# ConvFFN way down of a two-layer decoder trunk: block products in another order, accumulators of their own, and the next gate half placed ahead

## The chip, the cores and the metric

The kernel runs on one core of a Trainium2 chip. The metric is the device time of one execution in microseconds. A difference of 0.2% is about what a measurement of this kernel can tell from none.

## What is computed

Two decoder layers run over 512 positions of width 1024. Each layer adds three things to `x`: a mixer, a cross-attention, and a ConvFFN. Only the ConvFFN is touched by the change:

```python
def conv_ffn(h, w_up, conv_w, conv_b, w_down):
    S = h.shape[1]
    u = h @ w_up
    shift = lambda t, n: jnp.pad(t, ((0, 0), (n, 0), (0, 0)))[:, :S]
    u = sum(conv_w[CONV_WIDTH - 1 - n] * shift(u, n) for n in range(CONV_WIDTH)) + conv_b
    gate, up = jnp.split(u, 2, axis=-1)
    return (jax.nn.silu(gate) * up) @ w_down

    for l in range(DEPTH):
        ...
        x = x + conv_ffn(rms_norm(x, norm_ffn[l]), ffn_w_up[l], ffn_conv_w[l], ffn_conv_b[l], ffn_w_down[l])
```

The hidden width is 2816, that is 22 chunks of 128. All data are float32.

## The kernel before

**Arithmetic.** TensorE multiplies in a rounded 32-bit format. To keep float32 accuracy every operand is held as a high part (a ScalarE cast, line 213 for the helper `split`, line 171 for whole weight tiles) and a low part (VectorE subtracts the high part from the value, lines 214 and 172), and every product is three matmuls: high by high, high by low, low by high. Activations lie transposed: 128 features on the partitions, 512 positions along the row.

**The ConvFFN (`ffn`, line 578).** The 22 hidden chunks are worked in three parts of 8, 8 and 6 chunks. Inside a part the chunks come in pairs `m` (so a part has n = 4, 4 or 3 pairs). For each pair:

- the gate half: a weight tile of 1024 by 256 is loaded and split (`wload`), 2 times 24 matmuls of 512 columns go into one PSUM bank each (tag `pj`, 3 banks), and each bank is taken out by VectorE (line 585) and goes through the convolution: one ScalarE instruction (line 587) and two VectorE ones (588, 590), then the SiLU on ScalarE (601);
- the value half: the same with other weights, and a VectorE product with the gate (606);
- `seven` (line 314): from the two finished chunks it makes the seven right-hand factors of a seven-product block scheme for 2 by 2 blocks. Four VectorE instructions make sums (318 to 321), and `split` makes high and low parts in three steps: slot 0, slots 1 and 2, slots 3 to 6 of the tiles `s7h` and `s7l`.

**The way down (`seven_resid`, line 327).** After the pairs of a part the product with `w_down` follows, for two units `u` of 512 output features each. A unit loads two raw weight tiles (tag `wraw`, two buffers, shared with every other weight load), and makes seven weights out of them: `w11`, `w12` and `w22` are blocks of the raw tiles, `w1`, `w2`, `w4` and `w3` are sums, made by VectorE (`add`, line 348) in the tile `wsum` or in place. Each is split into parts held in the tiles `whi` and `wlo` (two buffers each, and each buffer holds two weights). A weight times its slot is a block product: `product` (line 350) issues 6n matmuls of 256 columns (line 357). With n = 4 a product is 24 matmuls, a unit 168 and a part 336; with n = 3 it is 18, 126 and 252. Over both layers the way down has 1848 of these matmuls.

The products go into three PSUM accumulators `al`, `be` and `de`, all with the tag `pj`. `into` (line 360) adds an accumulator to `x` with VectorE (line 362). The source order of a unit is w11 (al), w12 (be), w1 (de), w2 (al), w4 (de), w3 (al), w22 (al). The accumulator `al` keeps summing over four products, and is read by `into` after each of them, so the next matmul into `al` waits until that reading is over.

**What sets the order.** The code is written in source order and a scheduler then fixes, ahead of time, one order for each engine. Each engine works its own list strictly in that order and waits on semaphores where data or a buffer come from another engine. SyncE (SP) issues the weight loads. At the end of a part TensorE's list runs straight from the last value half to the first product of the way down, while the last pair's `seven` is still to be made.

**Names.** The profile's `wraw`, `whi`, `wlo`, `wsum`, `s7h`, `s7l`, `s7t`, `xT` (the residual `x`), `fu` and `fa` (the convolution's two tiles), and `ps_pj`, `ps_at`, `ps_ov`, `ps_tr` (PSUM banks by tag) are the program's own.

Of the kernel before, what the change touches and what calls it, by code (L numbers as in the profile page):

```python
# [33 lines left out]
def trunk(ctx, tc, x, mem, positions, norm_mix, norm_cross, norm_mem, norm_ffn,  # L34
# [292 lines left out]
    def seven_resid(w, r0, xs, u, tp, sums, after=None):  # L327

        n = len(xs)
        nk = 2 * n  # L330
        raws = []
        for i in range(2):
            raw = tl(wp, [P, KC, WCOL], "wraw", 2)
            SY.dma_start(out=raw[:, :nk], in_=wcols(w, r0, nk * P, (4 * u + 2 * i) * P))
            raws.append(raw)
        a11, a12 = (raws[0][:, i:nk:2] for i in range(2))
        a21, a22 = (raws[1][:, i:nk:2] for i in range(2))

        def parts():
            return tl(wp, [P, KC, WCOL], "whi", 2, FP32R), tl(wp, [P, KC, WCOL], "wlo", 2, FP32R)  # L340

        def put(t, i, src):
            h, lo = t[0][:, i * n:(i + 1) * n], t[1][:, i * n:(i + 1) * n]
            split(src, h, lo)
            return h, lo

        def add(out, a, b):
            V.tensor_tensor(out=out, in0=a, in1=b, op=ALU.add)  # L348

        def product(o, wt, slot, first):  # L350
            wh, wl = wt
            for j in range(2):
                c = slice(j * P, (j + 1) * P)
                for k in range(n):
                    xh, xl = xs[k][0][:, slot], xs[k][1][:, slot]
                    for i, (a, b) in enumerate(((wh, xh), (wh, xl), (wl, xh))):
                        T.matmul(o[:, j], lhsT=a[:, k, c], rhs=b, start=first and j == 0 and k == 0 and i == 0,  # L357
                                 stop=j == 1 and k == n - 1 and i == 2, skip_group_check=True)

        def into(i, th, o, op):  # L360
            x = xT2[2 * u + i][:, :, 256 * th:256 * th + 256]
            V.tensor_tensor(out=x, in0=x, in1=o, op=op)  # L362

        ta = parts()
        w11, w12 = put(ta, 0, a11), put(ta, 1, a12)
        ws = tl(tp, [P, KC // 2, WCOL], "wsum", sums)[:, :n]
        add(ws, a21, a22)
        al = ps("pj", 2, WCOL)
        product(al, w11, 0, True)
        be = ps("pj", 2, WCOL)  # L370
        product(be, w12, 1, True)
        tb = parts()
        w1 = put(tb, 0, ws)
        add(ws, ws, a11)
        w2 = put(tb, 1, ws)
        into(0, 0, al, ALU.add)
        into(0, 0, be, ALU.add)
        de = ps("pj", 2, WCOL)
        product(de, w1, 3, True)
        into(1, 1, de, ALU.subtract)  # L380
        product(al, w2, 4, False)
        into(0, 1, al, ALU.add)
        tc_ = parts()
        add(ws, ws, a12)
        w4 = put(tc_, 0, ws)
        add(a21, a11, a21)
        w3 = put(tc_, 1, a21)
        product(de, w4, 2, False)
        into(0, 1, de, ALU.add)
        product(al, w3, 5, False)  # L390
        into(1, 1, al, ALU.subtract)
        if after is not None:
            for c in (4 * u, 4 * u + 1):
                after(c)
        td = parts()
        w22 = put(td, 0, a22)
        product(al, w22, 6, False)
        into(1, 0, al, ALU.subtract)
        if after is not None:
            for c in (4 * u + 2, 4 * u + 3):  # L400
                after(c)
# [176 lines left out]
    def ffn(l, xp, sp):  # L578
# [14 lines left out]

        hs = {}

        def up_pair(m):
            gt = [None, None]

            def evg(j, o):
# [669 lines left out]
```

## Time and profile before

| | |
|---|---|
| median of 3 runs | 1644.17 us (1643.62 to 1646.21) |
| the profiled execution's own time | 1643.91 us |
| its span in the trace | 1642.2 us |
| TensorE (PE) busy | 1585.4 us, 97% |
| VectorE (DVE) busy | 1167.5 us, 71% |
| ScalarE (ACT) busy | 760.4 us, 46% |
| GpSimd (POOL) busy | 200.6 us, 12% |
| DMA | 145.71 MB, mean 89 GB/s |

The span goes from the first to the last instruction that the profiler saw; 1.7 us of the execution's own time lie outside it. PE's busy time says little by itself, since the ends of matmuls are modelled and overlap their successors. What counts is the distance from one matmul's start to the next one's: that is the pace, and whatever is above it is lost.

### The profile page before, as it was taken

The numbers are of one execution on the slowest core, as the hardware profiler recorded it, in microseconds if no ns is written. First come the engines' busy times: TensorE is split into PE (matmuls) and PEld (weight loads), VectorE is DVE, ScalarE is ACT, GpSimd is POOL, SyncE is SP. The second block draws the span as 40 slices with busy tenths as digits, with TensorE's granted clock in tenths as the row PEclk, the third lists the DMA queues.
The fourth block names the chain that finished last, engine by engine and source line by source line (L and its number), as shares of the span: only waits on it lengthen the run. The fifth ranks groups of instructions, "written<-read, shape, count | busy, mean of one in ns | idle before, by whom it ended". The sixth has DMA issues, their size and how long they took to land.

```text
span 1642.2 us, 23185 instructions
## 1 busy us (share of the span) xinstructions
PE 1585.4 (97%) x9182; PEld 1365.8 (83%) x9182; DVE 1167.5 (71%) x1888; ACT 760.4 (46%) x1312; POOL 200.6 (12%) x307
## 2 busy tenths in 40 slices
PE   8999999999998999998999999999999999998997
PEld 7977898887888888887789888988888879888877
DVE  6666966556788688688777676645564987787786
ACT  6576865444443443344433343543553543443342
POOL 3301421002000000001422223101011000000000
PEclk9999999999999999999999999999999999999999
DMA  6211433213222431311422123342112313221413
GB/s 189 78 53 35 128 104 125 78 52 103 77 77 71 135 103 52 129 64 39 129 78 78 52 79 102 103 154 92 63 52 77 103 58 129 96 78 54 152 39 90
DMA packets 144489, 145.71 MB, mean 89 GB/s; under 512 B 2844, under 2 KB 143837, under 8 KB 144381
## 3 DMA queue, kind: packets, MB, share of 16 engines
q1 hardware_dynamic: 143882, 143.98, 27.4%
q8 instruction: 73, 1.20, 0.3%
q0 software_dynamic: 96, 0.07, 0.1%
q14 instruction: 35, 0.29, 0.1%
q10 hardware_dynamic: 403, 0.18, 0.0%
HBM read 142.12 MB, written 2.10 MB: 88 GB/s over the span
## 4 chain that ended last, share of the span: by engine, by line
PE 85%; DVE 8%; ACT 3%; DMA 2%; issue 1%; POOL 1%; SPq 0%; ACTq 0%; DVEq 0%
PE ps_pj L184 22%; PE ps_pj L183 22%; PE ps_pj L185 22%; PE ps_pj L357 8%; DVE wlo L214 2%; PE ps_at L1091 2%; DVE xT L362 1%; DVE wsum L348 1%; DVE wlo L172 1%; ACT whi L213 1%; DVE s7l L214 1%; PE ps_ov L962 1%; DMA wraw<-in_ffn_w_down_dram 1%; DMA wraw<-in_ab_w_in_dram 1%; PE ps_tr L951 1%
## 5 line engine op out<-in xcount | busy, mean ns | idle before, releaser
L184 PE MATMUL ps_pj<-xl,whi 128*128 128x512 f32 x1088 | 433.4, 399 | 0.0
L183 PE MATMUL ps_pj<-xh,whi 128*128 128x512 f32 x1024 | 407.8, 399 | 0.0
L185 PE MATMUL ps_pj<-xh,wlo 128*128 128x512 f32 x1024 | 406.5, 398 | 0.0
L172 DVE TENSOR_TENSOR wlo<-wraw,whi 128x1024 fp32r<-128x1024 f32 (+1 forms) x228 | 266.1, 1199 | 42.7 <-ACT whi L171 42.1
L171 ACT CAST whi<-wraw 128x1024 fp32r<-128x1024 f32 (+1 forms) x228 | 219.6, 1013 | 139.7 <-PE ps_pj L184 94.2
L184 PEld LDWEIGHTS ps_pj<-xl,whi 128*128 128x128 f32 x1088 | 205.1, 188 | 47.2 <-issue 1.2
L183 PEld LDWEIGHTS ps_pj<-xh,whi 128*128 128x128 f32 x1024 | 193.1, 189 | 46.4 <-issue 1.2
L185 PEld LDWEIGHTS ps_pj<-xh,wlo 128*128 128x128 f32 x1024 | 192.9, 188 | 43.7
L357 PE MATMUL ps_pj<-s7h,whi 128*128 128x256 f32 x616 | 177.2, 290 | 17.3 <-DVE xT L362 8.2
L357 PE MATMUL ps_pj<-s7l,whi 128*128 128x256 f32 x616 | 175.7, 286 | 6.9 <-DVE s7l L214 6.9
L357 PE MATMUL ps_pj<-s7h,wlo 128*128 128x256 f32 x616 | 174.0, 286 | 5.6 <-DVE wlo L214 5.2
L357 PEld LDWEIGHTS ps_pj<-s7h,whi 128*128 128x128 f32 x616 | 118.0, 192 | 24.3 <-ACT s7h L213 8.8
L357 PEld LDWEIGHTS ps_pj<-s7l,whi 128*128 128x128 f32 x616 | 118.2, 192 | 9.7 <-DVE s7l L214 9.4
L357 PEld LDWEIGHTS ps_pj<-s7h,wlo 128*128 128x128 f32 x616 | 117.6, 192 | 7.7 <-DVE wlo L214 7.6
L246 POOL TENSOR_TENSOR nacc<-nacc,nsq 128x512 f32<-128x512 f32 x36 | 52.1, 1446 | 550.2 <-ACT nsq L245 549.8
L185 PE MATMUL ps_pj<-whi,xl 128*128 128x256 f32 x416 | 118.8, 288 | 0.1
L587 ACT ACTIVATE fa<-fu,ccol 128x512 f32<-128x512 f32 x88 | 71.6, 813 | 85.0 <-DVE fu L585 84.7
L585 DVE TENSOR_TENSOR fu<-ps_pj,rb 128x512 f32<-128x512 f32 x88 | 60.8, 691 | 62.9 <-PE ps_pj L185 62.8
L184 PE MATMUL ps_pj<-ol,whi 128*128 128x512 f32 x256 | 101.8, 398 | 0.0
L185 PE MATMUL ps_pj<-oh,wlo 128*128 128x512 f32 x256 | 101.4, 397 | 0.0
L183 PE MATMUL ps_pj<-oh,whi 128*128 128x512 f32 x256 | 100.0, 401 | 1.4 <-DVE xl L450 0.9
L362 DVE TENSOR_TENSOR xT<-xT,ps_pj 128x512 f32<-128x512 f32 x84 | 57.5, 685 | 43.9 <-PE ps_pj L357 43.7
(366 smaller groups left out, 2959.0 us busy)
## 6 DMA issues: line engine op xcount, KB each, us to landing
wraw<-in_ffn_w_up_dram SPq DMA_DIRECT2D x44, 1024.0 KB, 5.1
wraw<-in_xa_w_kv_dram SPq DMA_DIRECT2D x16, 1024.0 KB, 5.9
wraw<-in_ffn_w_down_dram SPq DMA_DIRECT2D x16, 1024.0 KB, 5.1
wraw<-in_hgrn_w_in_dram SPq DMA_DIRECT2D x16, 1024.0 KB, 5.4
wraw<-in_ab_w_in_dram SPq DMA_DIRECT2D x8, 1024.0 KB, 5.3
wraw<-in_xa_w_q_dram SPq DMA_DIRECT2D x8, 1024.0 KB, 5.2
wraw<-in_xa_w_o_dram SPq DMA_DIRECT2D x8, 1024.0 KB, 5.0
wraw<-in_ffn_w_down_dram SPq DMA_DIRECT2D x8, 768.0 KB, 4.4
```

What stands on the lines that cost most here:

```text
L171: A.copy(out=hi[:, k, c], in_=raw[:, k, c])
L172: V.tensor_tensor(out=lo[:, k, c], in0=raw[:, k, c], in1=f32(hi[:, k, c]), op=ALU.subtract)
L183: mm = T.matmul(o, lhsT=lh, rhs=rh, start=first, stop=False)
L184: T.matmul(o, lhsT=lh, rhs=rl, start=False, stop=False)
L185: T.matmul(o, lhsT=ll, rhs=rh, start=False, stop=last)
L214: V.tensor_tensor(out=lo, in0=src, in1=f32(hi), op=ALU.subtract)
L246: (V if c == KC - 1 else G).tensor_tensor(out=self.acc, in0=self.acc, in1=sq, op=ALU.add)
L357: T.matmul(o[:, j], lhsT=a[:, k, c], rhs=b, start=first and j == 0 and k == 0 and i == 0, stop=j == 1 and k == n - 1 and i == 2, skip_grou ...
L362: V.tensor_tensor(out=x, in0=x, in1=o, op=op)
L585: V.tensor_tensor(out=u, in0=o, in1=rb, op=ALU.mult)
L587: A.activation(out=a, in_=u, func=AF.Identity, scale=conv_col(l, 2, ch), bias=bias_col(l, ch))
L1091: T.matmul(po, lhsT=km[:, r * P:(r + 1) * P], rhs=skew(QP, h + r * P, (256 - h, 2), (2 * h, n2 // 2), (1, h)), start=True, stop=True)
```

## The change

- One function `seven_part` does both units. It has one order of products for most units ("fill") and another for the first unit of a layer's last part. In the fill order the products go w11 (al), w1 (de), w2 (al), w4 (de), w3 (al), w12 (be), w22 (al); in the other one w11 and w12 leave out their last pair at first, do it next, and then come w2, w1, w3, w4, w22.
- The accumulators get tags of their own: `al` has `at` (2 banks), `be` has `ov` (1 bank), `de` keeps `pj`. These tags were there before for attention's tiles.
- Inside a product the loop over pairs (k) is now outside and the one over the two column halves (j) inside. The matmul's line is 349 in the changed kernel (357 before), that of `into` is 366, that of `add` 353.
- A unit's first raw tile has a tile of its own, `wr`, with one buffer; the second still uses `wraw`. Splits of weights follow one another in pairs into a `whi` and `wlo` buffer over both units, so that a part takes 7 such buffers in a row where it took 8.
- The gate half of the next part's first pair is issued between the last value half and the way down. This holds for 4 of the 6 ways down; the last part of each layer has no next part.
- The tile `fa` has 6 buffers (4 before), `s7h` and `s7l` 4 (5 before).

The numbers of matmuls, casts, subtractions, sums, `into` instructions and loads stay the same. The diff, cut to its core:

```diff
-    def seven_resid(w, r0, xs, u, tp, sums, after=None):
+    def seven_part(w, r0, xs, sp, sums, fill, after=None):
...
+        def weights(src):
+            if side[1] == 0:
+                side[0] = tl(wp, [P, KC, WCOL], "whi", 2, FP32R), tl(wp, [P, KC, WCOL], "wlo", 2, FP32R)
+            h, lo = (t[:, side[1] * n:(side[1] + 1) * n] for t in side[0])
+            side[1] = 1 - side[1]
             split(src, h, lo)
             return h, lo
...
-            for j in range(2):
-                c = slice(j * P, (j + 1) * P)
-                for k in range(n):
-                    xh, xl = xs[k][0][:, slot], xs[k][1][:, slot]
...
+            for k in range(n) if ks is None else ks:
+                xh, xl = xs[k][0][:, slot], xs[k][1][:, slot]
+                for j in range(2):
+                    c = slice(j * P, (j + 1) * P)
...
+        def unit(u, fill):
+            raws = []
+            for i in range(2):
+                raw = tl(sp if i == 0 else wp, [P, KC, WCOL], "wr" if i == 0 else "wraw", 1 + i)
...
+            al, be, de = ps("at", 2, WCOL), ps("ov", 2, WCOL), ps("pj", 2, WCOL)
+            w11 = weights(a11)
+            if not fill:
+                w12 = weights(a12)
+                product(al, w11, 0, True, range(n - 1))
+                product(be, w12, 1, True, range(n - 1))
+                product(al, w11, 0, True, range(n - 1, n))
+                product(be, w12, 1, True, range(n - 1, n))
...
+                add(a21, a11, a21)
+                w3 = weights(a21)
+                w4 = weights(ws)
...
+            else:
+                add(ws, a21, a22)
+                w1 = weights(ws)
+                product(al, w11, 0, True)
+                product(de, w1, 3, True)
...
+                product(al, w3, 5, False)
+                w12 = weights(a12)
+                into(0, 1, de, ALU.add)
+                product(be, w12, 1, True)
+                w22 = weights(a22)
+                into(1, 1, al, ALU.subtract)
+                into(0, 0, be, ALU.add)
+            product(al, w22, 6, False)
...
+        unit(0, fill)
+        unit(1, True)
...
+        gt = gate_half(0)
         for a, b in parts:
             for m in range(a // 2, b // 2):
-                up_pair(m)
-            for u in range(2):
-                seven_resid(ffn_w_down[l], a * P, [hs[m] for m in range(a // 2, b // 2)], u, sp, 2 - l,
-                            (lambda c: store(sp, c)) if l == 1 and b == FC else None)
+                value_half(m, gt)
+                gt = gate_half(m + 1) if 2 * m + 2 < FC else None
+            seven_part(ffn_w_down[l], a * P, [hs[m] for m in range(a // 2, b // 2)], sp, 2 - l, gt is not None,
+                       (lambda c: store(sp, c)) if l == 1 and b == FC else None)
```

What this does to the engines' lists is seen at three places. The first is TensorE at the start of layer 0's first way down. Before, the last matmuls of the value half (512 columns) are followed at once by the product with `w11`:

```order
L184 MATMUL ps_pj_5114<-xl7_4515,whi_5075 128x512
L185 MATMUL ps_pj_5114<-xh7_4514,wlo_5076 128x512
L357 MATMUL ps_pj_5171<-s7h_4675,whi_5163 128x256 [waits DVE_49,Activation_49]
L357 MATMUL ps_pj_5171<-s7l_4676,whi_5163 128x256
L357 MATMUL ps_pj_5171<-s7h_4675,wlo_5164 128x256 [waits DVE_49]
```

In the changed kernel the same value half (it ends in `ps_pj_5114`) is followed by the next part's gate half, which writes `ps_pj_5167` and then `ps_pj_5199`:

```order
L184 MATMUL ps_pj_5114<-xl7_4515,whi_5075 128x512
L185 MATMUL ps_pj_5114<-xh7_4514,wlo_5076 128x512
L183 MATMUL ps_pj_5167<-xh0_4464,whi_5160 128x512 [waits DVE_49,Activation_49]
L184 MATMUL ps_pj_5167<-xl0_4465,whi_5160 128x512
L185 MATMUL ps_pj_5167<-xh0_4464,wlo_5161 128x512 [waits DVE_49]
```

And 48 matmuls later the way down begins, into an `at` bank:

```order
L184 MATMUL ps_pj_5199<-xl7_4515,whi_5160 128x512
L185 MATMUL ps_pj_5199<-xh7_4514,wlo_5161 128x512
L349 MATMUL ps_at_5236<-s7h_4675,whi_5239 128x256 [waits Activation_49]
L349 MATMUL ps_at_5236<-s7l_4676,whi_5239 128x256
L349 MATMUL ps_at_5236<-s7h_4675,wlo_5240 128x256 [waits DVE_49]
```

So 48 matmuls of 512 columns now stand between the last value half and the first block product.

The second place is the change from the first unit to the second in the same way down, again on TensorE. Before, w3 and w22 follow each other in one accumulator (`ps_pj_5171`), with a wait between them for `into`:

```order
L357 MATMUL ps_pj_5171<-s7l_5147,whi_5281 128x256
L357 MATMUL ps_pj_5171<-s7h_5146,wlo_5282 128x256
L357 MATMUL ps_pj_5171<-s7h_4675,whi_5339 128x256 [waits DVE_49,Activation_49]
L357 MATMUL ps_pj_5171<-s7l_4676,whi_5339 128x256
L357 MATMUL ps_pj_5171<-s7h_4675,wlo_5340 128x256
```

Now w3 ends in `ps_at_5236`, two matmuls each of the second unit's w11 (`ps_at_5445`) and w1 (`ps_pj_5447`) come in between, each waiting for a cast of its weights, and w22 follows in `ps_at_5236`:

```order
L349 MATMUL ps_at_5236<-s7l_5147,whi_5353 128x256
L349 MATMUL ps_at_5236<-s7h_5146,wlo_5354 128x256
L349 MATMUL ps_at_5445<-s7h_4675,whi_5409 128x256 [waits Activation_49]
L349 MATMUL ps_at_5445<-s7l_4676,whi_5409 128x256
L349 MATMUL ps_pj_5447<-s7h_4675,whi_5451 128x256 [waits Activation_49]
L349 MATMUL ps_pj_5447<-s7l_4676,whi_5451 128x256
L349 MATMUL ps_at_5236<-s7h_4675,whi_5409 128x256 [waits DVE_49]
L349 MATMUL ps_at_5236<-s7l_4676,whi_5409 128x256
```

The wait between two products in one accumulator has moved behind four matmuls, and two waits for ScalarE's casts stand ahead of them.

The third place is ScalarE at the start of layer 0's last part, which has no gate half to put ahead. Before, the last pair's three casts to `s7h` come first, and then the next weights (`whi_7192`, for w4 and w3), which wait for TensorE to leave a buffer:

```order
L213 CAST whi_7144<-wsum_7104 128x768 [waits DVE_49]
L213 CAST s7h_7081<-fa_7076 128x512 [waits DVE_49]
L213 CAST s7h_7081<-s7t_7083 128x1024 [waits DVE_49]
L213 CAST whi_7192<-wsum_7104 128x768 [waits PE_49]
L213 CAST whi_7192<-wraw_7096 128x768 [waits DMAHW7_49]
```

Now the two casts of weights (`whi_7190`, for w3 and w4) stand ahead of the last cast to `s7h`:

```order
L213 CAST whi_7143<-wsum_7094 128x768 [waits DVE_49]
L213 CAST s7h_7077<-fa_7072 128x512 [waits DVE_49]
L213 CAST whi_7190<-wraw_7092 128x768 [waits DMAHW7_49,PE_49]
L213 CAST whi_7190<-wsum_7094 128x768 [waits DVE_49]
L213 CAST s7h_7077<-s7t_7079 128x1024 [waits DVE_49]
```

The cast to slots 3 to 6 of `s7h` now stands behind a wait for TensorE.

More of the change, by code (lines that the diff above doesn't have):

```diff
@@ L325, in seven @@
         return hi, lo
-    def seven_resid(w, r0, xs, u, tp, sums, after=None):
+    def seven_part(w, r0, xs, sp, sums, fill, after=None):
         n = len(xs)
         nk = 2 * n
[L331 to L343, printed above, removed]
+        side = [None, 0]
+        def weights(src):
[3 more added lines that the diff above has]
+            side[1] = 1 - side[1]
@@ L344, in put, with product @@
             split(src, h, lo)
             return h, lo
-        def add(out, a, b):
-            V.tensor_tensor(out=out, in0=a, in1=b, op=ALU.add)
-        def product(o, wt, slot, first):
+        def product(o, wt, slot, first, ks=None):
             wh, wl = wt
-            for j in range(2):
-                c = slice(j * P, (j + 1) * P)
-                for k in range(n):
-                    xh, xl = xs[k][0][:, slot], xs[k][1][:, slot]
-                    for i, (a, b) in enumerate(((wh, xh), (wh, xl), (wl, xh))):
-                        T.matmul(o[:, j], lhsT=a[:, k, c], rhs=b, start=first and j == 0 and k == 0 and i == 0,
-                                 stop=j == 1 and k == n - 1 and i == 2, skip_group_check=True)
@@ L360, in into @@
[L360 to L401, printed above, removed]
+            for k in range(n) if ks is None else ks:
+                xh, xl = xs[k][0][:, slot], xs[k][1][:, slot]
+                for j in range(2):
+                    c = slice(j * P, (j + 1) * P)
+                    for i, (p, q) in enumerate(((wh, xh), (wh, xl), (wl, xh))):
+                        T.matmul(o[:, j], lhsT=p[:, k, c], rhs=q, start=first and k == 0 and j == 0 and i == 0,
+                                 stop=k == n - 1 and j == 1 and i == 2, skip_group_check=True)
@@ L594, in ffn, with gate_half @@
         hs = {}
-        def up_pair(m):
+        def gate_half(m):
             gt = [None, None]
@@ L602, in evg, with value_half @@
                 gt[j] = a
+            wg = wload(wcols(ffn_w_up[l], 0, D, m * WCOL))
+            proj_fm(wg, xh, xl, evg, n.finish if m == 0 else None, after_rows(n) if m == 0 else None)
+            return gt
+        def value_half(m, gt):
             def evu(j, o):
```

50 lines of the change are left out of this document (46 added, 4 removed).

## The prediction

> **What bounds the kernel now.** I read the page first: the engines' busy time and the chain of work that ended last.
>
> ```profile
> span 1642.2 us, 23185 instructions
> PE 1585.4 (97%) x9182; PEld 1365.8 (83%) x9182; DVE 1167.5 (71%) x1888; ACT 760.4 (46%) x1312; POOL 200.6 (12%) x307
> ...
> PE 85%; DVE 8%; ACT 3%; DMA 2%; issue 1%; POOL 1%; SPq 0%; ACTq 0%; DVEq 0%
> ```
>
> TensorE carries 85% of that chain. The change takes no matmul away, so all it can save is time between matmuls. For that I need the pace. In the timeline of TensorE ahead of the first way down, 15 steps of 512 columns take 3.50 us (0.233 each), and inside the way down a 256-column step takes 0.118:
>
> ```profile
> 489.71 0.40 PE L185 MATMUL ps_pj<-xh,wlo 128*128 128x512 f32 x1
> ...
> 493.21 0.40 PE L185 MATMUL ps_pj<-xh,wlo 128*128 128x512 f32 x1
> ...
> 514.69 0.28 PE L357 MATMUL ps_pj<-s7l,whi 128*128 128x256 f32 x1
> 514.81 0.28 PE L357 MATMUL ps_pj<-s7h,wlo 128*128 128x256 f32 x1
> 515.96 0.36 PE L357 MATMUL ps_pj<-s7h,whi 128*128 128x256 f32 x1 [0.87 <-DVE xT L362]
> ```
>
> The last of these rows is the first matmul of w22. It came 1.15 us after its predecessor, 1.03 over the pace, since `into` had to read the accumulator first. Next, the table by stage: the six ways down, line 357 alone (second column: stretch, then PE busy and count; the number after PEld is the granted clock).
>
> ```profile
> 493.40:540.20 46.80, 42.57 (x336) 40.48 (x335) 1.00 0.27 90
> 629.90:676.30 46.40, 42.09 (x336) 40.06 (x335) 1.00 0.28 91
> 743.40:786.40 43.00, 34.81 (x252) 32.91 (x252) 0.92 0.27 84
> 1343.10:1389.90 46.80, 42.61 (x336) 40.50 (x335) 1.00 0.28 91
> 1479.50:1527.60 48.10, 43.58 (x336) 41.78 (x335) 0.96 0.27 88
> 1594.80:1633.60 38.80, 32.86 (x252) 30.66 (x251) 1.00 0.22 69
> sum 269.90, PE 238.52 PEld 226.39; mean PE 39.75 PEld 37.73
> ```
>
> At the pace, 336 matmuls take 39.6 us and 252 take 29.7. So the six lose 7.2, 6.8, 13.3, 7.2, 8.5 and 9.1 us; of the last, some 2.3 are other matmuls, the transposes of the output. Together that is about 50 us, 3% of the span, and it is all that this change can reach. What it consists of is in the answer for line 357 (idle time before its weight loads, by what ended it; microseconds and times):
>
> ```profile
> DVE s7l L214: 16.3, 24
> ACT s7h L213: 15.5, 20
> DVE wlo L214: 12.8, 16
> DVE xT L362: 10.6, 19
> ACT whi L213: 7.7, 13
> ```
>
> Of the 62.9 us in these rows (more than the loss, since weight loads run ahead of their matmuls) 31.8 wait for `s7h` and `s7l`, the factors of the part's last pair. The timeline at a part's start shows it:
>
> ```profile
> 498.92 0.36 PE L357 MATMUL ps_pj<-s7h,whi 128*128 128x256 f32 x1 [0.27 <-DVE xT L362]
> ...
> 500.08 0.38 PE L357 MATMUL ps_pj<-s7h,whi 128*128 128x256 f32 x1 [0.69 <-ACT s7h L213]
> ...
> 504.39 0.51 PE L357 MATMUL ps_pj<-s7h,whi 128*128 128x256 f32 x2 [0.64 <-ACT s7h L213]
> ```
>
> The chain behind it, on VectorE and ScalarE, with the durations that I use below:
>
> ```profile
> 498.09 0.68 DVE L362 TENSOR_TENSOR xT<-xT,ps_pj 128x512 f32<-128x512 f32 x1
> 498.69 0.69 DVE L606 TENSOR_TENSOR fa<-fa 128x512 f32<-128x512 f32 x1
> 499.29 1.22 DVE L214 TENSOR_TENSOR wlo<-wsum,whi 128x1024 fp32r<-128x1024 f32 x1
> 500.43 0.42 DVE L319 SCALAR_TENSOR_TENSOR s7t<-s7t,fa 128x256 f32<-128x256 f32 x1
> ...
> 504.37 1.23 DVE L214 TENSOR_TENSOR s7l<-s7t,s7h 128x1024 fp32r<-128x1024 f32 x1 [1.11 <-ACT s7h L213]
> ```
>
> ```profile
> 503.29 1.05 ACT L213 CAST s7h<-s7t 128x1024 fp32r<-128x1024 f32 x1 [3.26 <-DVE s7t L321]
> 504.24 1.04 ACT L213 CAST whi<-wsum 128x1024 fp32r<-128x1024 f32 x1
> 505.19 1.04 ACT L213 CAST whi<-wraw 128x1024 fp32r<-128x1024 f32 x1
> ```
>
> The value half ended at 493.4 and its last factor was complete at 505.6, 12.2 us later, because the subtractions and sums for the weights stand between on VectorE. A cast follows a cast after 0.95 us.
>
> **The four filled ways down.** Here 48 matmuls of 0.233, 11.2 us, go ahead of the first block product. They are not extra: the gate half is only done earlier. I set T = 0 at the first block product and walk the changed order with the durations above. VectorE's queue after the value half holds the two subtractions for w11 and w1 (1.22 each), the convolution and `seven`. The last evacuation of the gate half (line 585 before, as long as the 0.69 of line 606) comes free at T = 0, and the last `s7l` (1.23) stands right behind it, so it is complete at 1.9. It is first wanted in the second product's last quarter, at 2.83 + 2.12 = 4.95, since a product is 24 times 0.118 = 2.83. All stalls on `s7h` and `s7l` go, with 3 us to spare. w2's subtraction ends at 3.1, `into` for `al` at about 4.5, and w2 starts at 5.7: that wait goes as well.
>
> What is late next is weights, because there are two `whi` buffers. w3 and w12 share the one that w11 and w1 leave at 5.7; two casts (1.9) and two subtractions behind a sum and an `into` end at 9.4, and w12 wants its low part at 8.7 to 8.9: about 0.45 lost. At the unit's end w22 and the next w11 share the buffer that w4 leaves at 15.9, so they are cast by 17.8; TensorE arrives at 17.4 and waits some 0.5. The next w1 needs the buffer that w3 leaves at 17.4, and is cast third, by 18.9: another 0.85, with 0.2 of hand-over. Sum at the boundary 1.55. Inside the second unit I leave 0.4, like one of the present waits for `wlo`. That makes 2.4 lost in each way down of layer 0; the slightly other order of layer 1 gives 2.0. Before it was 7.2 + 6.8 + 7.2 + 8.5 = 29.7, after 8.8: **gain 20.9 us**. After the way down only the value half's weights must be ready; their buffer is left by w3, two products (5.7) ahead, and two casts and two subtractions (1.9 and 2.4, overlapping) fit. The accumulators' own banks, the loop order and the smaller `seven` pool I cost at nothing: the same matmuls at the same pace, covered by a free bank each; if that cover fails, one `into` (0.68 and its hand-over, 1.03 above) per unit shows up, up to 12 us in all.
>
> **The single raw tile `wr`.** The second unit's first load waits until the first unit is done with it, at w12's subtraction (T = 9.4). DMA rows for these loads:
>
> ```profile
> wraw<-in_ffn_w_down_dram SPq DMA_DIRECT2D x16, 1024.0 KB, 5.1
> ...
> wraw<-in_ffn_w_down_dram SPq DMA_DIRECT2D x8, 768.0 KB, 4.4
> ```
>
> It lands at 14.5; its first cast is due at 16.9. So 2.4 us of cover in the filled parts. Queued behind it on SP are the second `wraw` and the next value half's weights.
>
> **The two unfilled ways down.** In layer 0's last one ScalarE now casts w3 and w4 ahead of the last `s7h`, and these casts wait for `be`'s product to leave the buffer. From there: two casts of 768 columns (about 0.75 apart), one of 1.05, and hand-overs: 2.9 us of idle TensorE, then the 1.23 of `s7l`, of which about 1.0 shows. The waits of the start that remain are two, 0.85 and 0.70. On VectorE a sum for the second unit stands ahead of an `into`, and waits for `wr`'s DMA, about 1.4. The worst wait of today has a successor of the same kind:
>
> ```profile
> 763.70 1.87 DVE L348 TENSOR_TENSOR wsum<-wraw 128x768 f32<-128x768 f32 x1 [0.95 <-DMA wraw<-in_ffn_w_down_dram]
> ...
> 768.15 0.58 PE L357 MATMUL ps_pj<-s7h,wlo 128*128 128x256 f32 x1 [2.43 <-DVE wlo L214]
> ```
>
> I leave 2.6 for it. Sum 9.4 against 13.3.
>
> The clock matters here. In three stretches the granted clock was halved (the number behind the counts):
>
> ```profile
> 750.10:753.50 3.40, 2.86 (x15) 2.66 (x14) 2.29 (x5) 1.10 (x2) 0.00 (x0) 0.57 0.19 30
> 767.60:771.00 3.40, 2.85 (x13) 2.85 (x14) 2.83 (x4) 1.40 (x4) 0.00 (x0) 0.50 0.02 5
> 1487.80:1491.20 3.40, 3.27 (x15) 3.27 (x16) 1.54 (x3) 1.14 (x2) 0.00 (x0) 0.50 0.31 69
> ```
>
> Each is 3.4 us long and holds 15 or 16 steps where 29 would fit; at full pace they are 1.9 us, so each costs about 1.5. They follow clusters of waits, each under 2.5 us. The 9.4 has none in it; a wait of 2.9 will bring one, so 10.9, **gain 2.4**. [...]
>
> In layer 1's last part I find waits of 1.3, 1.1, 1.0, 1.3 and 1.0, together 5.7 against 9.1 − 2.3 = 6.8: **gain 1.0**, rounded.
>
> **The sum.** 20.9 + 2.4 + 1.0 = 24.3 off the span of 1642.2 gives 1617.9. The profiled execution took 1643.91, 1.7 more than its span, and the median is 1644.17, 0.3 more again: 1619.9, so I forecast **1620**. If the clock stays up it is 1.5 less (1618.5); with a perfectly free boundary in the four filled parts (8.8 gone) 33 are gained (1611). If the chains err by 1 us per way down each, 18 are gained (1626).
>
> **Rivals.**
>
> *Weights become the bound.* Seven pairs of weights pass two buffers in a part. If each of the seven recyclings shows the 0.85 that I find at the boundary, a filled way down loses 6.0, not 2.2: 4 × 3.8 = 15 less, 9 gained, **1635**. For it: `wlo` and `whi` already make 20 us of the idle time, and VectorE is busy 71%. Against: most recyclings have two products, 5.7 us, for 1.9 of casts and 2.4 of subtractions.
>
> *The clock falls in each way down.* Short waits at bank changes bunch and bring one stretch of 1.5 in five ways down where I have none: 7.5 less, **1627.5**. [...] The trace has one such stretch in the four long ways down, with more waits than I expect.
>
> *The change does not pay.* The stall moves from `s7h` to the boundary or behind the way down in full: within 3.3 us of **1644**. Against it stands the walk above: the two chains use different buffers.
>
> *The single `wr` makes it slower.* Place: the second unit's first cast on ScalarE and its first sum on VectorE, six times. If the load is issued only when the whole first unit has left the tile and nothing covers it, TensorE waits 5.1 + 1.05 + 1.23 = 7.4 six times, 44 us, less the 24.3 gained: 20 slower, **1664**. It decides from a wait of 4.1 us per way down on (24.3 / 6). For it: one buffer, and `wr` is queued on SP with others. Against: w12's subtraction comes 7.5 us before the next cast is due.
>
> **Numbers.** Chances: my forecast (1612 to 1628) 0.70, the clock 0.08, the weights 0.12, no change 0.04, `wr` 0.06. The range 1613 to 1633 leaves out the last two, part of the weights' case and the best corner, some 2 in 10. Faster by over 0.2% (3.3 us) 0.90, within it 0.04, slower 0.06.
>
> **What would show it.** After the gate half no waits for `s7h` or `s7l` in the four filled ways down; each of these 41 to 43 us long; at the unit boundary waits for `whi` of 0.5 and 0.9; in layer 0's last part one wait for `s7h` near 2.9 and a halved clock behind it. I am wrong if a filled way down takes over 45 us, if the chain of waits names `wr`, or if time is lost ahead of the value halves.

## The result, and the profile after

| | before | changed |
|---|---|---|
| median, us | 1645.04 (1643.62 to 1646.21, 4 runs) | 1617.75 (1615.94 to 1618.62, 4 runs) |
| span of the profiled execution, us | 1642.2 | 1616.3 |

The ratio is 0.9833 (95% interval 0.9816 to 0.9850). The forecast was 1620, in the range 1613 to 1633. The page of the changed kernel has the same work on TensorE in a shorter span, and TensorE now makes 90% of the chain that ended last, where it was 85%:

```profile
span 1616.3 us, 23124 instructions
PE 1576.8 (98%) x9182; PEld 1363.9 (84%) x9182; DVE 1164.2 (72%) x1888; ACT 761.1 (47%) x1312; POOL 196.2 (12%) x307
...
PE 90%; DVE 4%; ACT 3%; DMA 1%; POOL 1%; issue 0%; SPq 0%; DVEq 0%; ACTq 0%
```

The table of the six ways down (line 349; first the stretch and its length, after PEld the granted clock):

```profile
503.00:544.50 41.50, 40.62 (x336) 39.92 (x335) 1.00 0.35 107
634.10:675.70 41.60, 40.73 (x336) 39.95 (x335) 1.00 0.32 100
731.70:776.00 44.30, 36.02 (x252) 34.73 (x251) 0.85 0.21 66
1338.30:1380.00 41.70, 40.82 (x336) 40.26 (x335) 1.00 0.34 105
1469.70:1511.40 41.70, 40.83 (x336) 40.25 (x335) 1.00 0.31 99
1567.40:1607.50 40.10, 34.54 (x252) 32.97 (x251) 0.91 0.16 47
```

The four filled ways lost 29.5 us over the pace before (46.8, 46.4, 46.8 and 48.1 long) and lose 8.0 now. The two last ways, which have no gate half ahead, got longer: 44.3 after 43.0, and 40.1 after 38.8, and their granted clock is down to 0.85 and 0.91. What ends the idle time before the weight loads of these matmuls (all six ways, in us and times) has turned round; the largest group is now `whi`:

```profile
ACT whi L213: 15.0, 12
ACT s7h L213: 9.9, 8
...
```

TensorE at the start of layer 0's first way: the gate half's last matmul is followed by the first block product after one step, with no wait.

```profile
502.77 0.40 PE L185 MATMUL ps_pj<-xh,wlo 128*128 128x512 f32 x1
503.01 0.28 PE L349 MATMUL ps_at<-s7h,whi 128*128 128x256 f32 x1
```

On VectorE at the same place the last `s7l` ends at 505.0, which is T = 2.0 in the prediction's count, and `into` ends at 507.4, T = 4.4; what needs them comes later (at 5.0, and at 5.8 where 5.7 was forecast):

```profile
503.81 1.22 DVE L214 TENSOR_TENSOR s7l<-s7t,s7h 128x1024 fp32r<-128x1024 f32 x1
...
506.75 0.68 DVE L366 TENSOR_TENSOR xT<-xT,ps_at 128x512 f32<-128x512 f32 x1
```

TensorE's list is not in the source's order: in layer 0 `w12` begins fourth, at 511.65 (T = 8.6), and `w4` and `w3` follow it, mixed. That is the order in the prediction's walk. The two waits of this way that are left are both where the second unit's weights are cast:

```profile
521.11 0.39 PE L349 MATMUL ps_at<-s7h,whi 128*128 128x256 f32 x1 [0.43 <-ACT whi L213]
...
522.05 0.39 PE L349 MATMUL ps_pj<-s7h,whi 128*128 128x256 f32 x1 [0.44 <-ACT whi L213]
```

In layer 1 the scheduler's order is another one: there the filled ways have no wait at the boundary, but two inside the second unit (0.70 for a `wlo` and 0.50 for `into`, over the pace, in each).

Where the 25.9 us of span went, as time over the pace (the distance between matmul starts, less 0.234 or 0.118 each):

| stretch | before | changed | gain | forecast |
|---|---|---|---|---|
| four filled ways | 29.5 | 8.0 | 21.4 | 20.9 |
| layer 0's last way | 13.2 | 14.5 | −1.3 | 2.4 |
| layer 1's last way | 6.7 | 8.4 | −1.7 | 1.0 |
| up to the first way | 7.4 | 5.8 | 1.6 | 0 |
| between the layers' ways (norm, mixer, attention, first pairs) | 9.5 | 3.9 | 5.6 | 0 |

So the sum of the prediction came out for its main term, and two errors elsewhere cancelled: 6.4 us too much hoped for in the two last ways, 7.2 us gained where no change was forecast. That they cancelled is luck. The experiments ask which part of the change made the main term, what the last ways lost, and where the 7.2 came from.

### The profile page after: what moved, and what is told of

Its sections match the earlier page's. It is cut to its first block, busy times and chain, and to the rows that moved or that the text cites. A ratio compares the mean times of both kernels' runs of the same rounds, so it can differ in the third digit from the quotient of the medians.

```text
span 1616.3 us, 23124 instructions
## 1 busy us (share of the span) xinstructions
PE 1576.8 (98%) x9182; PEld 1363.9 (84%) x9182; DVE 1164.2 (72%) x1888; ACT 761.1 (47%) x1312; POOL 196.2 (12%) x307
## 4 chain that ended last, share of the span: by engine, by line
PE 90%; DVE 4%; ACT 3%; DMA 1%; POOL 1%; issue 0%; SPq 0%; DVEq 0%; ACTq 0%
PE ps_pj L185 23%; PE ps_pj L184 23%; PE ps_pj L183 23%; PE ps_at L349 7%; PE ps_pj L349 3%; PE ps_ov L349 2%; PE ps_at L1123 1%; DVE wlo L214 1%; PE ps_ov L994 1%; ACT whi L213 1%; DVE xl L236 1%; DMA wraw<-in_ab_w_in_dram 1%; PE ps_tr L983 1%; PE ps_at L183 1%; PE ps_at L185 1%; DVE wlo L172 1%
## 5 line engine op out<-in xcount | busy, mean ns | idle before, releaser
L172 DVE TENSOR_TENSOR wlo<-wraw,whi 128x1024 fp32r<-128x1024 f32 (+1 forms) x228 | 264.2, 1191 | 45.8 <-ACT whi L171 45.2
L183 PEld LDWEIGHTS ps_pj<-xh,whi 128*128 128x128 f32 x1024 | 192.7, 188 | 44.6 <-issue 1.2
L349 PE MATMUL ps_at<-s7h,whi 128*128 128x256 f32 x352 | 102.7, 292 | 5.8 <-ACT s7h L213 3.4
L349 PE MATMUL ps_at<-s7l,whi 128*128 128x256 f32 x352 | 102.0, 290 | 1.5 <-DVE s7l L214 1.5
L349 PE MATMUL ps_at<-s7h,wlo 128*128 128x256 f32 x352 | 101.8, 290 | 1.3 <-DVE wlo L214 1.3
L183 PE MATMUL ps_pj<-whi,xh 128*128 128x256 f32 x288 | 82.8, 290 | 0.7 <-ACT xh L235 0.7
L184 PE MATMUL ps_pj<-wlo,xh 128*128 128x256 f32 x288 | 81.9, 286 | 0.0
L185 PEld LDWEIGHTS ps_pj<-whi,xl 128*128 128x128 f32 x416 | 78.5, 190 | 0.6 <-DVE xl L236 0.3
L349 PEld LDWEIGHTS ps_at<-s7h,whi 128*128 128x128 f32 x352 | 69.3, 197 | 7.8 <-ACT s7h L213 3.8
```

Of the source, the lines that this page charges most:

```text
L172: V.tensor_tensor(out=lo[:, k, c], in0=raw[:, k, c], in1=f32(hi[:, k, c]), op=ALU.subtract)
L183: mm = T.matmul(o, lhsT=lh, rhs=rh, start=first, stop=False)
L184: T.matmul(o, lhsT=lh, rhs=rl, start=False, stop=False)
L185: T.matmul(o, lhsT=ll, rhs=rh, start=False, stop=last)
L349: T.matmul(o[:, j], lhsT=p[:, k, c], rhs=q, start=first and k == 0 and j == 0 and i == 0, stop=k == n - 1 and j == 1 and i == 2, skip_grou ...
```

## The experiments

My theory was that the gate half put ahead is what pays, that the new order and the accumulators' banks add little, and that in the last ways the new order costs. The rivals were that order and banks pay, and, for the 5.6 us between the layers, that they are the clock's chance. Each kernel ran beside the kernel before; the ratio is to that one.

**1. The gate half ahead alone**, on the kernel before:

```diff
...
-                up_pair(m)
+                value_half(m, gt)
+                gt = gate_half(m + 1) if 2 * m + 2 < FC else None
             for u in range(2):
                 seven_resid(ffn_w_down[l], a * P, [hs[m] for m in range(a // 2, b // 2)], u, sp, 2 - l,
```

> The kernel before with the next part's first gate half put ahead of four ways down (and fa 6, seven 4 buffers), order of products, accumulators and raw tiles as before. My theory (the gate half ahead is what pays): in the four filled ways the waits for s7h and s7l at the start go and the wait between w3 and w22 (1.03) and those of the second unit (about 1.3) stay, so each takes about 42.3 us where before took 46.4 to 48.1 and the changed kernel 41.5 to 41.8; the two last ways stay at 43.0 and 38.8; gain 17 to 19 in the ways down, 1626 us if nothing moves outside them. Rival (order and accumulators pay): the four stay at 45 us or more, 1637 to 1643 us.

1622.33 us, ratio 0.9877 (0.9862 to 0.9892). Its six ways:

```profile
504.50:546.80 42.30, 40.84 (x336) 40.02 (x336) 1.00 0.31 100
636.30:678.30 42.00, 40.67 (x336) 39.85 (x336) 1.00 0.31 101
734.20:781.20 47.00, 35.95 (x252) 34.15 (x252) 0.89 0.25 79
1343.50:1385.80 42.30, 40.84 (x336) 40.02 (x336) 1.00 0.31 101
1475.30:1517.60 42.30, 41.00 (x336) 40.17 (x336) 1.00 0.32 100
1573.50:1612.20 38.70, 33.70 (x252) 31.66 (x251) 0.96 0.23 69
```

The filled ways are 42.0 to 42.3 us, as my theory had it: the gate half alone makes 19.6 of the 21.4 us (29.5 against 9.9 left). It missed one thing: layer 0's last way, whose code is the old one, took 47.0 in place of 43.0. The stretch after it lost 4.0 where it had lost 9.5. The scheduler moved more of the next layer's norm into the last way (its trace has twelve `xl` instructions there, before has eight), so the two have to be counted together: 22.7 before, 21.2 here, 18.4 in the changed kernel. Of the 2.8 between the last two, 2.9 lie at the end of the mixer's first projections (experiment 5) and not in the way.

**2. Everything but the gate half ahead**: each part calls `value_half(m, gate_half(m))` and all first units use the order for unfilled starts.

```diff
-        gt = gate_half(0)
...
-                value_half(m, gt)
-                gt = gate_half(m + 1) if 2 * m + 2 < FC else None
-            seven_part(ffn_w_down[l], a * P, [hs[m] for m in range(a // 2, b // 2)], sp, 2 - l, gt is not None,
+                value_half(m, gate_half(m))
+            seven_part(ffn_w_down[l], a * P, [hs[m] for m in range(a // 2, b // 2)], sp, 2 - l, False,
```

> The changed kernel without the gate half ahead (every first unit in the order for unfilled starts). My theory: each start waits for the last pair's factors as before, and ScalarE casts weights ahead of them, so a way of four pairs takes 46 to 48 us and the time is 1641 to 1648 us, no change from before. Rival (order and accumulators pay): ways of 43 us or less, 1625 to 1632 us.

1644.53 us, ratio 1.0002 (0.9992 to 1.0011): no change. Its first way takes 46.0 us, with the wait that ScalarE's turned order makes:

```profile
506.51 0.38 PE L349 MATMUL ps_at<-s7h,whi 128*128 128x256 f32 x1 [2.91 <-ACT s7h L213]
508.15 0.56 PE L349 MATMUL ps_at<-s7l,whi 128*128 128x256 f32 x1 [1.14 <-DVE s7l L214]
```

Order, banks and the tile `wr` without the gate half give nothing. That settles the main question for my theory.

**3. The last parts as before**: `seven_resid` with its raw tiles and banks is called where `gt is None`, `seven_part` elsewhere.

```diff
...
+            if gt is not None:
+                seven_part(ffn_w_down[l], a * P, xs, sp, 2 - l, True)
+            else:
+                for u in range(2):
+                    seven_resid(ffn_w_down[l], a * P, xs, u, sp, 2 - l, (lambda c: store(sp, c)) if l == 1 else None)
```

> The changed kernel with the way down of before (order, accumulators, raw tiles) in the two last parts only. The two last ways took 44.25 and 40.0 us in the changed kernel and 43.0 and 38.8 before. My theory (the changed order costs 3 us there): they go back to 43.0 and 38.8, and the time is 3 us below the changed kernel's, 1615, if the stage between the layers keeps its 5.6 us. Its list of instructions there is nearer to that of before: if the 5.6 us hang on that order, they are lost again and the time is about 1620; if they hang on chance in the clock, they come and go from run to run.

1621.39 us, ratio 0.9864 (0.9850 to 0.9879): my theory had it 3 us faster than the changed kernel, and it is not faster. Layer 1's last way took 39.3, layer 0's 46.3, and that one loses 16.6 over the pace in place of 14.5. But as in experiment 1 more of the next layer's norm stands in it (twelve `xl` instructions, eight in the changed kernel), and the norm's wait behind it is 0.8 in place of 2.2. So way and norm have to be counted together. From the start of the way to the 80th matmul behind it, where the norm is done, it is 65.3 us here, 66.2 in the changed kernel (67.9 when it was run again, experiment 5) and 66.1 before. By these profiles the changed order costs 1 to 2.6 us in layer 0's last way, of which the clock may be part; in layer 1's the 39.3 lie between the changed kernel's two profiles (40.0 and 38.9), which shows no difference. The profile's span is 3.3 longer than the changed kernel's for reasons elsewhere: 2.9 at the end of the mixer's first projections, whose order is that of before, 1.2 up to the first way and 1.0 in the second.

**4. The fill order everywhere**, `fill` always true.

```diff
-            seven_part(ffn_w_down[l], a * P, [hs[m] for m in range(a // 2, b // 2)], sp, 2 - l, gt is not None,
+            seven_part(ffn_w_down[l], a * P, [hs[m] for m in range(a // 2, b // 2)], sp, 2 - l, True,
```

> The changed kernel with the fill order in the last parts too, which have nothing ahead. My theory: w1 is second and needs slot 3 of the last pair some 3.5 us into the way, while it is complete about 10 us after the value half, so TensorE stands 5 to 8 us, the two last ways take 48 to 52 and 44 to 48 us, and the time is 1624 to 1632 us. Rival (the order of products does not matter at the start): within 2 us of the changed kernel.

1625.13 us, ratio 0.9887 (0.9871 to 0.9904). The direction was right and the time is in the range, but the place is not: the last ways took 44.6 and 41.4, not 48 to 52 and 44 to 48. TensorE waits for the last pair's factors in layer 0's way, which starts at 734.05:

```profile
742.69 0.38 PE L349 MATMUL ps_pj<-s7h,whi 128*128 128x256 f32 x1 [2.61 <-ACT s7h L213]
743.95 0.38 PE L349 MATMUL ps_pj<-s7l,whi 128*128 128x256 f32 x1 [0.76 <-DVE s7l L214]
```

The factors did come some 10 us after the value half (`s7l` lets TensorE go at 9.9, in layer 1's way at 11.0). What I had wrong is when TensorE gets there: 5.9 and 6.3 us into the way, not 3.5, since the scheduler put twelve matmuls of another product ahead, which themselves wait 0.8 and 1.2. So it stands 2.8 and 0.9 over the pace at these two rows, 3.4 and 0.9 in layer 1's way. The rest of the loss is between the layers (7.8 in place of 3.9).

**5. The changed kernel once more.**

> The changed kernel once more, unaltered, beside the next ones on the same chip. If the 5.6 us won between layer 0's last way down and layer 1's first hang on the order of instructions (the order theory), this profile shows 3.5 to 4.5 us over the pace there again, the time is 1616 to 1619, and the start up to the first way loses the same 5.8. If part of them is the clock's chance (the clock theory), both stretches come out other by multiples of about 1.5 us, up to 7.5 and 7.4.

1618.77 us, ratio 0.9839 (0.9824 to 0.9854). Between the layers 4.0 again, up to the first way 5.4. All profiles together sort by the order of instructions: at the end of the mixer's first projections the kernels with the order of before (before, and experiments 1 to 4 and 9) have two waits of 1.14 and 1.82, those with the order of the changed kernel (it, 5 to 8 and 10) two of 0.90 and 0.80. The table by stage around this place, first of the kernel before (the granted clock is the third number from the end):

```profile
1010.00:1016.00 6.00, 3.71 (x29) 3.15 (x27) 5.82 (x10) 4.83 (x10) 3.63 (x4) 1.00 0.00 0
1016.00:1022.00 6.00, 5.62 (x31) 5.26 (x32) 5.07 (x15) 2.82 (x8) 0.93 (x2) 0.72 0.69 200
```

The same two stretches in the changed kernel:

```profile
997.00:1003.00 6.00, 4.39 (x34) 3.65 (x33) 5.82 (x11) 4.76 (x10) 3.18 (x4) 1.00 0.00 0
1003.00:1009.00 6.00, 5.83 (x41) 5.22 (x42) 5.95 (x18) 3.76 (x10) 0.00 (x0) 1.00 0.68 200
```

Behind the larger waits the clock fell (0.72 over 6 us), behind the smaller ones it stayed (1.00). (Experiment 10 has the smaller ones and fell to 0.72 there all the same, so this is likelier with the one order, not certain.) The same 300 matmuls there (the 1300th to the 1600th behind layer 0's last way) take 48.7 us before and 48.5 to 49.7 in experiments 1 to 4 and 9, but 46.2 to 46.3 in the changed kernel and in 5 to 8, and 47.5 in 10. So 2.4 of the 5.6 us come from a reordering of the mixer that the diff doesn't name. Another 1.9 come from the mixer's start (the 80th to the 400th matmul, 54.8 us before, 52.9 in the changed kernel). There only the kernel before has these two waits on TensorE:

```profile
819.37 1.16 PE L1071 MATMUL ps_at<-hQ,hK 128*128 128x128 f32 x8 [0.50 <-DVE hQ L1153]
...
825.70 0.69 PE L1091 MATMUL ps_at<-hQ,KM 128*128 128x128 f32 x4 [0.72 <-DVE hQ L1074]
```

The last 1.1 is a shorter wait in the norm (3.33 to 2.22 over the pace), and it is no net gain: layer 0's last way and the norm together are 66.1 us before and 66.2 in the changed kernel. The 1.6 us up to the first way are the clock: before has a halved stretch at 102.0 to 105.4 (granted clock 0.50), the changed kernel has 1.00 there, and experiments 1, 7 and 10, which have the changed kernel's instructions up to the first way, lose 7.2 to 7.3, as before did.

**6. The factor's cast first**: in the unfilled order the casts of w3 and w4 are held behind the last cast to `s7h`.

```diff
...
                 w3 = weights(a21)
+                behind(last_cast[1], last_cast[0])
                 w4 = weights(ws)
+                behind(last_cast[1], last_cast[0])
```

> The changed kernel with the casts of w3 and w4 in the two unfilled ways held behind the last cast to s7h. My theory (that inversion on ScalarE makes the waits of 2.65 and 0.98 in layer 0's last way and 1.03 and 1.00 in layer 1's): the 2.65 goes to below 0.8, layer 0's last way gets 1 to 3 us shorter than 44.25, unless two matmuls that now stand ahead of w3 wait for wr instead (then they show a wait of 1 to 2 us); time 1614 to 1617. Rival (the factor is late by VectorE's chain anyway): the wait stays at 2.5 under another name, same time.

1616.65 us, ratio 0.9831 (0.9814 to 0.9847). Layer 0's last way:

```profile
741.78 0.38 PE L352 MATMUL ps_at<-s7h,whi 128*128 128x256 f32 x1 [1.42 <-ACT s7h L213]
743.04 0.38 PE L352 MATMUL ps_at<-s7l,whi 128*128 128x256 f32 x1 [0.76 <-DVE s7l L214]
746.08 0.58 PE L352 MATMUL ps_at<-s7h,whi 128*128 128x256 f32 x1 [1.60 <-ACT whi L213]
```

The inversion is 1.1 of that wait: 2.65 over the pace became 1.58, not below 0.8, and 1.75 came back as the expected wait for the weights of the next unit. The way took 43.5 us (44.3 and 45.8 in the changed kernel's two profiles). Layer 1's took 38.2 (40.0 and 38.9); there the 1.03 is gone, the 1.00 became 0.91, and a wait of 0.62 for `into` came up. What is left of the 2.65, I take it, is the chain to the last pair's factors itself; that was not tried further.

**7. The next layer's norm held back**, behind the last weight cast of layer 0's last way.

```diff
-                A.activation(out=a, in_=v, func=AF.Copy, scale=g)
+                ins = A.activation(out=a, in_=v, func=AF.Copy, scale=g)
+                if self.fold:
+                    behind(ins, last_cast[1])
...
```

> The changed kernel with the next layer's norm (its casts and squares on ScalarE, and with them its work on VectorE and GpSimd) held behind the last weight cast of layer 0's last way. My theory (the wait of 4.45 for w4 comes from VectorE's xl instructions that stand ahead of the sum and run beside GpSimd at 0.75 to 1.5 us a piece in place of 0.48): the 4.45 goes to below 1, the way is 39.5 to 41 us long in place of 44.25, and the stretch after it pays 1 to 4 us back; sum of both 1 to 3.5 us less, 1614 to 1617. Rival (the single tile wr holds the sum up): the 4.45 stays.

1616.14 us, ratio 0.9823 (0.9808 to 0.9837). This is about the largest single wait of the changed kernel, in layer 0's last way. TensorE's waits there, in the changed kernel:

```profile
742.49 0.44 PE L349 MATMUL ps_at<-s7h,whi 128*128 128x256 f32 x1 [2.48 <-ACT s7h L213]
743.82 0.58 PE L349 MATMUL ps_at<-s7l,whi 128*128 128x256 f32 x1 [0.68 <-DVE s7l L214]
...
765.28 0.58 PE L349 MATMUL ps_pj<-s7h,whi 128*128 128x256 f32 x1 [4.29 <-ACT whi L213]
```

The cast that it waits for, on ScalarE, waits for a sum:

```profile
764.40 0.83 ACT L213 CAST whi<-wsum 128x768 fp32r<-128x768 f32 x1 [2.92 <-DVE wsum L353]
```

VectorE ahead of that sum (the last row):

```profile
755.40 0.48 DVE L236 SCALAR_TENSOR_TENSOR xl<-xT,gcol,xh 128x256 fp32r<-128x256 f32 x1
755.80 0.68 DVE L366 TENSOR_TENSOR xT<-xT,ps_at 128x512 f32<-128x512 f32 x1
...
759.59 1.51 DVE L236 SCALAR_TENSOR_TENSOR xl<-xT,gcol,xh 128x256 fp32r<-128x256 f32 x1
761.02 0.67 DVE L366 TENSOR_TENSOR xT<-xT,ps_pj 128x512 f32<-128x512 f32 x1
761.62 1.87 DVE L236 SCALAR_TENSOR_TENSOR xl<-xT,gcol,xh 128x256 fp32r<-128x256 f32 x2
763.42 0.94 DVE L353 TENSOR_TENSOR wsum<-wsum,wr 128x768 f32<-128x768 f32 x1
```

And GpSimd in the same microseconds:

```profile
755.68 1.37 POOL L246 TENSOR_TENSOR nacc<-nacc,nsq 128x512 f32<-128x512 f32 x1 [340.82 <-ACT nsq L245]
759.32 1.50 POOL L246 TENSOR_TENSOR nacc<-nacc,nsq 128x512 f32<-128x512 f32 x1 [2.27 <-ACT nsq L245]
761.56 1.26 POOL L246 TENSOR_TENSOR nacc<-nacc,nsq 128x512 f32<-128x512 f32 x1 [0.74 <-ACT nsq L245]
```

The sum for w4 stands behind the norm's `xl` on VectorE, and these run beside GpSimd's additions: 1.51 for one and 1.87 for two that take 0.48 apiece where no addition runs (753.75 and 754.14). With the norm held the 4.29 is gone, and the way takes 37.5 us in place of 44.3 (39.5 to 41 were expected), by the table of the held kernel:

```profile
735.70:773.20 37.50, 32.66 (x252) 31.41 (x251) 0.95 0.25 78
```

The stretch after it gives 2.5 back (6.4 in place of 3.9). So the profile has 4.3 less in both; the second way down took part of that back (4.4 over the pace, not 2.0: a wait of 0.77 for `into`, and a stretch of 3.4 us at half clock behind it). The medians differ by 1.6 and 2.6 from the two of the changed kernel. That the intervals overlap leaves the size open; that the norm's work on the three engines made the wait is shown by the row that vanished when it was held.

**8. The accumulators back in `pj`.**

```diff
-            al, be, de = ps("at", 2, WCOL), ps("ov", 2, WCOL), ps("pj", 2, WCOL)
+            al, be, de = ps("pj", 2, WCOL), ps("pj", 2, WCOL), ps("pj", 2, WCOL)
```

> The changed kernel with all three accumulators back in the tag pj (3 banks). My theory (banks of their own are worth nothing when nothing waits for a free bank): filled ways 41.4 to 42.2 us as before, time within 2 us of the changed kernel. Rival (the own banks are what lets the gate half go ahead): the first product or the next value half waits for a pj bank, each filled way 1 us longer or more, 4 us or more in all.

1618.98 us, ratio 0.9841 (0.9826 to 0.9855), filled ways of 41.4, 41.7, 41.8 and 41.7 us. The changed kernel, run beside it, had 0.9839 (experiment 5). The banks of their own are worth nothing here.

**9. The first raw tile back in the ring.**

```diff
-                raw = tl(sp if i == 0 else wp, [P, KC, WCOL], "wr" if i == 0 else "wraw", 1 + i)
+                raw = tl(wp, [P, KC, WCOL], "wraw", 2)
```

> The changed kernel with the first raw tile of a unit back in the ring of two wraw tiles. My theory (the own tile is needed because the fill order reads the first raw tile until w12, its sixth product): the second unit's raw tiles can only be loaded when w12 and w22 have been split, so 5.1 of load, a sum and a split stand between, and each filled way shows a wait of 3 to 6 us at the second unit; ways of 44 to 47 us, time 1628 to 1640. Rival (two tiles do, as in the kernel with only the gate half ahead): ways of 42 us, 1617 to 1621.

1652.18 us, ratio 1.0051 (1.0038 to 1.0065): slower than the kernel before, and by more than expected. TensorE at the second unit of the first way:

```profile
529.80 0.38 PE L349 MATMUL ps_pj<-s7h,whi 128*128 128x256 f32 x1 [1.26 <-ACT whi L213]
531.66 0.39 PE L349 MATMUL ps_pj<-s7h,wlo 128*128 128x256 f32 x1 [1.36 <-DVE wlo L214]
```

VectorE at the same place, the sum for the second unit's w1:

```profile
527.39 1.22 DVE L353 TENSOR_TENSOR wsum<-wraw 128x1024 f32<-128x1024 f32 x1 [0.70 <-DMA wraw<-in_ffn_w_down_dram]
```

The second unit's sum waits for its load, and the cast and the subtraction behind it keep TensorE. The filled ways take 47.2 to 49.3 us, 26.1 over the changed kernel's; the waits themselves are within what I expected, 0.58, 0.57, 1.42, 1.52 and 0.48 over the pace in the first way, 4.6 together, but the granted clock falls behind them (0.96 and 0.97 in all four ways, 1.00 in the changed kernel). The other 8 us lie outside the filled ways: 4.3 between the layers, 2.8 in the two last ways and 0.9 up to the first.

**10. Three holds together**: those of 6 and 7, and the second unit's first matmuls held behind the first unit's w4 in the unfilled ways.

```diff
...
                         mm = T.matmul(o[:, j], lhsT=p[:, k, c], rhs=q, start=first and k == 0 and j == 0 and i == 0,
...
+                        if first and side[2] is not None:
+                            behind(mm, side[2])
```

> The changed kernel with three holds in the unfilled ways: the casts of w3 and w4 behind the last cast to s7h, the next layer's norm behind the last weight cast, and the second unit's first matmuls behind the first unit's w4. My theory: the waits of 4.45 and 1.75 are gone, 2.65 becomes about 1.6; layer 0's last way takes 35.5 to 37.5 us (44.25 in the changed kernel), the stretch after it gives back about 2.4, layer 1's last way 38 to 38.5; 6 to 7 us less over the pace than the changed kernel, of which the clock's stretches take some, so 1611 to 1615. Rival (the clock takes it all back, as it nearly did when the norm alone was held): 1616 to 1618.

1615.87 us (1612.55 to 1618.15, 5 runs), ratio 0.9822 (0.9806 to 0.9839). The last ways are 38.2 and 38.0 us (35.5 to 37.5 and 38 to 38.5 were expected), 8.1 less together. The wait of 4.45 is gone and 2.65 became 1.58, but the 1.75 is still there as 2.13, now for `into`. The stretch between the layers rose to 8.5, the start to 7.3 by the clock, and the second way to 43.9 by the clock and a wait of 0.65 for `into`. So the time missed the 1611 to 1615. It is the lowest median of all, but not separable from the changed kernel's 1617.75 and 1618.77 by these intervals.

## Why the prediction was right or wrong, point by point

- *The filled ways* (gain 20.9): measured 21.4. The first `s7l` was forecast for T = 1.9 and came at 2.0, `into` for 4.5 and came at 4.4. The two waits at the unit boundary were forecast at 0.5 and 0.85 with 0.2 of hand-over; they are 0.58 and 0.60 over the pace (layer 0; in layer 1 the waits are inside the second unit). The wait for w12's low part (0.45) was only 0.16. Experiments 1 and 2 show that the gate half ahead does it; the new order adds 1.8 us to it in the four ways.
- *The accumulators, the loop order and the pools at nothing*: right for the banks by experiment 8. The loop order was not tried by itself.
- *The single tile `wr`*: in the first way the load lands at T = 14.6 (forecast 14.5). VectorE waits for it in each filled way (1.5 to 2.9 us) and ScalarE in layer 1's, but no wait of TensorE and no step of the chain that ended last names `wr` there, so the cover held. The rival had the sign wrong: the tile is a condition of the new order of products, and without it the time is 34 us longer (experiment 9). With the old order the ring of two was enough (experiment 1).
- *Layer 0's last way* (waits 9.4, one halved stretch, gain 2.4): the waits add up to 9.8 (0.80, 2.65, 0.98, 0.36, 4.45, and two steps of 0.26 that no other engine ended), of which 2.65 and 0.98 for the factor were forecast as 2.9 and 1.0. The step that failed is the clock: "a wait of 2.9 will bring one" stretch of 3.4 us at 1.5. There were two, with more steady work in each (the third line is layer 1's last way):

```profile
744.00:749.40 5.40, 5.40 (x25) 5.39 (x26) 4.07 (x5) 1.57 (x2) 0.00 (x0) 0.50 0.04 10
765.60:770.00 4.40, 4.40 (x22) 4.40 (x22) 2.41 (x4) 1.10 (x2) 0.00 (x0) 0.50 0.17 40
1579.80:1585.80 6.00, 6.00 (x28) 5.75 (x29) 4.64 (x6) 1.56 (x2) 0.00 (x0) 0.50 0.01 1
```

  At half clock a step of 256 columns takes 0.213, so 45% of such a stretch is lost: 2.4 and 2.0 here. (The 3.4 us at 1.5 came from three stretches of the kernel before, said to hold 15 or 16 steps each; the second holds 13, with a wait in it.) One more miss was hidden in the right sum: I had 1.4 for `wr`'s load and 2.6 for a later wait; it was one wait of 4.45, and its cause was not a DMA but the norm's work on VectorE beside GpSimd (experiment 7).
- *Layer 1's last way* (waits 5.7, gain 1.0): the waits are 5.6, and the third line above, 6.0 us at half clock, cost 2.7 that I had at nothing.
- *Outside the ways at nothing*: wrong by 7.2. I had held the order there for equal in cost. The scheduler's other order in the mixer made 4.3: 1.9 at its start, where two waits of 0.66 and 0.88 over the pace went, and 2.4 at the end of its first projections, where 1.3 of waits went and a clock stretch behind them. The 1.6 at the start is the clock's. The last 1.1 is the shorter wait in the norm, paid for in layer 0's last way (experiment 5).
- *Rivals*: weights became the first thing late, as that rival said, at 2.0 per way and not 6.0. The clock fell in no filled way of the changed kernel's first profile (granted clock 1.00 in all four), and with one tag for all accumulators or three the filled ways are the same (41.4 to 41.8 us in experiment 8, 41.5 to 41.7 here). So no run shows that short waits at bank changes bring a stretch of 1.5 in five ways, the 7.5 of that rival. In experiments 7 and 10 the clock did fall once in the second way (granted clock 0.96 over the way in experiment 7).

## What to carry to other kernels

Where an engine that works in order stands at the end of a stage because the last item's preparation is not done, look for work of the next stage that needs none of it, and issue it first; here 48 matmuls covered a chain of 12 us four times. When the order inside the stage is changed as well, see which buffer now lives longer: the new order of products without the tile of its own lost all of the gain and more, while the old order did without. Count the waits of a way down and the clock's answer to them apart, since in the ways that still wait the second was about half the first (4.4 beside 9.8, 2.7 beside 5.6). Look at stages that the diff doesn't touch, since a scheduler may order them anew, and count a stage together with the next one when work moves between them.

## What the runs showed of the hardware that I had not expected

- The granted clock was halved for 3.4 or 6.8 us at a time, or up to the end of the trace; TensorE was busy for 6.12 and 4.72 us of the two stretches of 6.80 below. In the changed kernel, layer 0's last way, around the falls at 742.7 and 763.2 (after the length of the stretch, TensorE's busy time and count; the granted clock is the third number from the end):

```profile
739.30:742.70 3.40, 0.92 (x7) 0.71 (x7) 3.40 (x6) 2.51 (x3) 0.00 (x0) 1.00 0.37 109
742.70:749.50 6.80, 6.12 (x28) 5.82 (x28) 5.14 (x6) 1.57 (x2) 0.00 (x0) 0.50 0.22 72
759.80:763.20 3.40, 1.19 (x11) 0.99 (x9) 3.40 (x4) 0.63 (x1) 2.28 (x2) 0.99 0.00 0
763.20:770.00 6.80, 4.72 (x22) 4.72 (x23) 4.81 (x8) 2.30 (x3) 0.00 (x0) 0.50 0.11 26
```

  In the profiles of the kernel before and of the changed kernel each fall lies a whole multiple of 3.413 us behind the one ahead of it: here 20.48, six times; 9, 230 and 10 times behind that in the changed kernel, and 190, 5, 11, 62, 138 and 44 times in the kernel before (seven falls, from 102.0 to 1638.0). Equal waits were not answered alike. Two profiles of the same instructions (the changed kernel and experiment 5) have the same waits of 2.65, 0.98 and 4.4 in layer 0's last way and the same two falls of 6.8 us, but 5.4 and 4.4 us of them lie behind the waits, in steady work, in one and 5.4 and 5.7 in the other; in layer 1's last way the fall lasts 6.8 us in one and 3.4 in the other. So the same stage differs by 1.1 to 1.6 us between two runs (in layer 0's, 0.9 of a wait for `into` in the second of them included). Behind three waits of 0.58, 0.60 and 0.77 within 2.1 us the clock fell in experiment 7 (0.50 from 656.6 to 660.0), while behind 0.60, 0.61 and 0.83 at the same place it did not in experiment 5. Before the two falls above TensorE was busy for 0.92 and 1.19 us of 3.4. What makes the clock fall was not shown.
- The norm's `xl` on VectorE (128x256, from `xT` and `xh` in SBUF) took longer where GpSimd's addition had begun first. In the changed kernel it took 0.93, 1.51, 1.48 and 1.51 us (at 756.40, 759.59, 761.62 and 781.50, which is 0.72, 0.27, 0.07 and 0.19 behind the start of an addition), and each time it ended 0.28 after the addition's end (761.10 and 760.82 for the second). It took 0.48 where it began first (755.40, GpSimd 755.68), as where no addition ran (753.75). `into`, with an operand in PSUM, began 0.12 us after an addition (755.80) and kept its 0.68 (0.67 at 757.25, with none).
